# A two-layer hybrid encoder in fp32 products: projections read the tokens interleaved, in a regular order

## The chip, the cores and the metric

The kernel runs on one core of one Trainium2 chip. The metric is the device time of one execution in microseconds (us). The kernel before was run three times: 2403.81, 2404.59 and 2405.13 us, median 2404.59.

## The reference

A trunk of two layers works on one sequence of 256 tokens of width 2048, all in float32. Layer 0 mixes tokens with two recurrences (RWKV-7 heads and an RG-LRU), layer 1 with sparse attention. Around the mixers stand large projections, which are nearly all of the arithmetic:

```python
for layer in range(DEPTH):                       # 2
    if layer % 2 == 0:
        z = x @ ev_w_in[j]                       # 2048 -> 5408
        y = concatenate([rwkv7_mix(z[..., :A_COLS], ...), rglru_mix(z[..., A_COLS:], ...)]) @ ev_w_out[j]
    else:
        y = dsa_mix(x, od_w_in[j], ...) @ od_w_out[j]
    x = layer_norm(DN_ALPHA * x + y, ln1_g[layer], ln1_b[layer])
    x = layer_norm(DN_ALPHA * x + conv_ffn(x, ffn_w_up[layer], ...), ...)   # 2048 -> 11264 -> 5632 -> 2048
    x = x + sigmoid(x @ ple_w_gate[layer]) * (p[layer] @ ple_w_proj[layer])
```

`rwkv7_mix` first shifts by a token: `z = z + (token_shift(z) - z) * mu`, where `token_shift` moves every token one place to the right and puts zero in front. `rglru_mix` and `conv_ffn` begin with a causal depthwise convolution over 4 and 3 tokens. So three consumers of projections look at neighbouring tokens.

## The kernel before

**Layout.** Activations are held transposed: features on the 128 partitions, the S = 256 tokens along the free dimension. A block of 128 features is one tile of 512 numbers, called `x`, `y`, `g` or `o` after the stage: its first 256 columns are the rounded high part of the 256 tokens (type fp32r), its last 256 the low part, which is what the rounding left over. Weights are split in the same way, per chunk of 1024 columns (eight 128x128 blocks): `wchunk` (L117) loads a chunk `raw`, ScalarE writes `hi` (L131), VectorE writes `lo` = raw - hi (L132). In the profile both show at L53, the wrapper that gives them priority.

**Products.** One block of a projection, in float32 accuracy, is three products: high weight by high activation, high weight by low activation, low weight by high activation. `mm3` (L141) issues them in one of two forms.
- As a pair: one matmul of 512 columns, `hi` by the whole tile (L149), whose two halves of sums lie in the two halves of a bank, then one of 256 columns, `lo` by the high part (L150). Here L149 is called H and L150 L. The consumer adds the two halves.
- As a triple, with `one=True`: three matmuls of 256 columns into the same half bank (L145, L146, L147). The consumer finds a finished sum.

Each matmul has its own weight load (LDWEIGHTS) of 128 columns. A row of a projection, 128 output features, is 16 blocks (44 in the down projection) accumulated into one PSUM bank; `gproj` (L171) runs over the row in groups of eight blocks. Banks come from three pools, whose tiles the trace names `pp` and `a`.

**An order by hand.** `dodge` (L152) gives some rows another order of their 32 matmuls, which `ordered` (L164) issues; they stand at L169. In the first such row the second half is eight H, then eight L; in the row after it blocks 12 and 13 are issued H, H, L, L, and all others as pairs. These two rows come after the first five rows of each up projection and again every 29 rows (`DODGE`), after the first five rows of each gate projection, and at the start of the attention output projection.

**Stages.** Layer 0: the input projections in triples, filled with the small matmuls of the recurrences by a scheduler that orders by priority (span to about 380 us); the output projection; LayerNorm. Then, in both layers, the up projection of 88 rows with its convolution and gate (`ffn`, L376), the down projection of 16 rows (L400 to L409), LayerNorm, the gate projection of 16 rows (`ple`, L464). Layer 1 has the attention before that. Right after a LayerNorm, `head` (L219) issues the first five (or three) rows block by block as the normalised tiles arrive.

**Consumers of a bank.** `evac` (L246): ScalarE copies the second half out (L250), VectorE adds the first half to it (L251). `ln_set` and `ln_more` (L267, L276) add a row's sums to the residual. `shifted` (L732) scales a sum on ScalarE (L737) and adds `mu` times its left neighbour on VectorE (L738). `rglru` (L1023) writes the last tap of its convolution on ScalarE (L1028) and adds three more taps on VectorE, reading the bank three times (L1031). Smaller ones are at L447, L451, L480, L1063, L1277, L1322 and L1352.

Of the kernel before, what the change touches and what calls it, by code (L numbers as in the profile page):

```python
# [14 lines left out]
P = 128  # L15
D = 2048
S = 256
# [3 lines left out]
ALPHA = 4.0 ** 0.25  # L21
# [35 lines left out]
class Core:  # L57
# [77 lines left out]
    def hl_split(self, dst, src):  # L135
# [2 lines left out]
        nc.scalar.copy(dst[:, 0:S], src)  # L138
        nc.vector.tensor_tensor(dst[:, S:2 * S], src, dst[:, 0:S].bitcast(F32), op=ALU.subtract)  # L139

    def mm3(self, ps, hi, lo, hl, first, last, one=False):  # L141

        nc = self.nc
        if one:
            nc.tensor.matmul(ps[:, 0:S], hi, hl[:, 0:S], start=first, stop=False)  # L145
            nc.tensor.matmul(ps[:, 0:S], hi, hl[:, S:2 * S], start=False, stop=False)  # L146
            nc.tensor.matmul(ps[:, 0:S], lo, hl[:, 0:S], start=False, stop=last)  # L147
            return
        nc.tensor.matmul(ps[:, 0:2 * S], hi, hl, start=first, stop=False)  # L149
        nc.tensor.matmul(ps[:, 0:S], lo, hl[:, 0:S], start=False, stop=last)  # L150

    def dodge(self, j):  # L152


        self.order = None
        if j in (0, 1):
            o = [(c, k) for k in range(KD) for c in "HL"]
            if j == 0:
                o[16:] = [(c, k) for c in "HL" for k in range(8, KD)]
            else:  # L160
                o[24:28] = [(c, k) for c in "HL" for k in (12, 13)]
            self.order = o

    def ordered(self, ps, hi, lo, hls, k0, order):  # L164

        for what, k in order[2 * k0:2 * k0 + 16]:
            c = slice((k - k0) * P, (k - k0 + 1) * P)
            out, w, x = (ps[:, 0:2 * S], hi, hls[k]) if what == "H" else (ps[:, 0:S], lo, hls[k][:, 0:S])
            self.nc.tensor.matmul(out, w[:, c], x, start=(what, k) == order[0], stop=(what, k) == order[-1], skip_group_check=True)  # L169

    def gproj(self, src, hls, group=8, one=False, more=None):  # L171
# [74 lines left out]
    def evac(self, ps, out):  # L246

        nc = self.nc
        t = self.t("ev")
        nc.scalar.copy(t, ps[:, S:2 * S])  # L250
        nc.vector.tensor_tensor(out, ps[:, 0:S], t, op=ALU.add)  # L251


    def ln_begin(self, new=None):
# [12 lines left out]
    def ln_set(self, m, ps, hl):  # L267

        nc = self.nc
        s = self.sm[m] = self.ln_new(m)  # L270
        t = self.t("lnt")
        nc.vector.scalar_tensor_tensor(s, hl[:, 0:S].bitcast(F32), ALPHA, ps[:, 0:S], op0=ALU.mult, op1=ALU.add)
        nc.vector.scalar_tensor_tensor(t, hl[:, S:2 * S].bitcast(F32), ALPHA, ps[:, S:2 * S], op0=ALU.mult, op1=ALU.add)
        nc.vector.tensor_tensor(s, s, t, op=ALU.add)

    def ln_more(self, m, ps):  # L276

        s = self.sm[m]
        self.nc.vector.tensor_tensor(s, s, ps[:, 0:S], op=ALU.add)

    def ln_stat(self, m):

# [144 lines left out]
    def ple_proj(self, l, wps, phl, half, pool=None):  # L427

        pps, pss = [], [None] * 2
        for m in range(8 * half, 8 * half + 8):  # L430
            wp = wps[m % 8 // 4]
            if pool is None:

                if m % 4 < 2:
                    pss[m % 2] = self.ps()
                ps, n = pss[m % 2], m % 4 // 2
            else:
                if m % 2 == 0:
                    ps = self.ps()
                n = m % 2  # L440
            pv = ps[:, n * S:(n + 1) * S]
            for k in range(2):
                o = ((m % 4) * 2 + k) * P
                self.mm3(pv, wp[0][:, o:o + P], wp[1][:, o:o + P], phl[k], k == 0, k == 1, True)
            if pool is None:
                t = self.t("sp")
                self.nc.scalar.mul(t, pv, 0.5)  # L447
                self.nc.sync.dma_start(self.spill[l][:, (m % 8) * S:(m % 8 + 1) * S], t)
            elif m % 2:
                pp = pool.tile([P, 2 * S], F32, tag="pp", name=self.nm("pp"), bufs=KD // 2)  # L450
                self.nc.scalar.mul(pp, ps, 0.5)  # L451
                pps += [pp[:, 0:S], pp[:, S:]]
        return pps

# [9 lines left out]
    def ple(self, l, pool, new, raws, emit):  # L464

        nc = self.nc
        V = nc.vector
        wps = self.ple_weights(l, 0)
        x, pps, first = self.head(wps, l, 0, [self.a[f"pg{l}"][m] for m in range(FIRST)], f"ln2g{l}", f"ln2b{l}", new, raws, pool)
        pps += self.ple_back(l, pool)  # L470

        def finish(m, ps):

            b = self.t("pl_b")
            pp = pps[m]
            V.tensor_tensor(b, pp, x[m][:, 0:S].bitcast(F32), op=ALU.add)
            V.tensor_tensor(b, b, x[m][:, S:].bitcast(F32), op=ALU.add)
            g = self.t("pl_g")
            if m == KD - 1:
                nc.scalar.activation(g, ps[:, 0:S], AF.Tanh, scale=0.5)  # L480
# [198 lines left out]
class Even:  # L679
# [343 lines left out]
    def rglru(self, j, yout):  # L1023
        nc, k = self.nc, self.k
        V, A, T = nc.vector, nc.scalar, nc.tensor
        ps = yield from k.gproj(k.a["evin"][27 + 2 * j], self.x, one=True)
        xc = self.r1("xc")
        A.activation(xc, ps[:, 0:S], AF.Identity, bias=k.v("bconv_b", j), scale=k.v("bconv3", j))  # L1028
        for n in range(3):
            d = 3 - n  # L1030
            V.scalar_tensor_tensor(xc[:, d:], ps[:, 0:S - d], k.v(f"bconv{n}", j), xc[:, d:], op0=ALU.mult, op1=ALU.add)  # L1031
        bw = self.R.tile([P, 256], F32, tag="bw", name=k.nm("bw"), bufs=1)
        nc.sync.dma_start(bw, k.a["bw"][j])
        rest = k.gproj(k.a["evin"][28 + 2 * j], self.x, one=True)
# [28 lines left out]
        A.activation(g, ps[:, 0:S], AF.Gelu_apprx_tanh)  # L1063
        V.tensor_tensor(h, h, g, op=ALU.mult)
        k.hl_split(yout, h)

# [171 lines left out]
class Odd:  # L1238
# [31 lines left out]
    def index_keys(self):  # L1270
# [6 lines left out]
        A.copy(z, ps[:, 0:S])  # L1277
        yield
        ps = self.a1()
        for i in range(2):  # L1280
# [26 lines left out]
    def low_rank(self, m0, n, gain, name, back=False):  # L1307


        nc, k = self.nc, self.k  # L1310
        V, A = nc.vector, nc.scalar
        zt = self.R.tile([P, 4 * S], F32, tag="bias", name=k.nm("lz"), bufs=2)
        zs = [zt[:, i * S:(i + 1) * S] for i in range(n)]
        acc = k.t("rms")
        for i in range(n):
            g = k.gproj(k.a["odin"][m0 + i], self.x, one=True)
            for _ in range(8):
                next(g)
            yield
            ps = drain(g)  # L1320
            z = zs[i]
            A.copy(z, ps[:, 0:S])  # L1322
            if i == 0:
                A.activation(acc, z, AF.Square)
            else:
                q = k.t("rq")
                A.activation(q, z, AF.Square)
                V.tensor_tensor(acc, acc, q, op=ALU.add)
            yield
        R = k.group_pow(acc, P, 1.0 / (n * P), 1e-6, ALU.add, self.a1, k.t)  # L1330
        yield
        R = k.tok_bcast(R, P, k.t("grb"), "a1")
        out = []
        for i in range(n):
            zn = k.t("zn")
            src, r = zs[i], R[:, 0:S]
            if back:
                src, r = src[:, ::-1], r[:, ::-1]
            V.scalar_tensor_tensor(zn, src, k.v(gain, i), r, op0=ALU.mult, op1=ALU.mult)
            o = self.R.tile([P, 512], F32R, name=f"{name}{i}")  # L1340
            k.hl_split(o, zn)
            out.append(o)
        return out

    def small_proj(self, w, o, hls, out, scale=1.0):
# [6 lines left out]
        nc.scalar.mul(out, ps[:, 0:S], scale)  # L1352

    def scores(self):

# [261 lines left out]
```

## Time and profile before

| | |
|---|---|
| median of three runs | 2404.59 us (2403.81 to 2405.13) |
| span of the profiled execution | 2404.5 us; no other time is recorded for it |
| granted TensorE clock | 1.000 |
| TensorE, matmuls | 2382.8 us busy (99%), 15064 instructions |
| TensorE, weight loads | 2139.0 us (89%) |
| VectorE | 1773.9 us (74%) |
| ScalarE | 1377.4 us (57%) |
| GpSimd | 77.0 us (3%) |
| DMA | 433.77 MB, mean 180 GB/s |

In the rows of the profile "PE" is a matmul and "PEld" a weight load. Matmuls are pipelined: the duration in a row holds the way through the array, so that two of 0.40 and 0.28 us overlap, and what a matmul costs is the distance from its start to the start of the next. A row of the timeline gives start and duration in us, then engine, line, operation, the names of output and inputs, the stationary size, the shape that moves, and how many such instructions it merges. A row of the windows gives a stretch of the span and its length, then for each engine the busy time and in brackets the number of instructions, the granted clock, the share of the DMA engines and GB/s.

### The profile page before, as it was taken

To read this page: it belongs to the slowest core of one execution; us is meant where nothing else is said; L and a number is where in the kernel's file an instruction comes from. 1 tells how busy PE (TensorE), PEld (TensorE's weight loads), DVE (VectorE), ACT (ScalarE), POOL (GpSimd) and SP (SyncE) were. 2 spreads that over 40 slices of the span, in tenths; PEclk is the share of its full clock that TensorE was granted. 3 is DMA by queue.
4 is the path that set the end of the run, shared out by engine and by line. 5 is a ranking of instruction groups with operands and counts; after the bars stand their busy time and mean duration, and the time that the engine had idled before them with its cause. 6 is when DMAs were issued, how large, how long until landed. Compare 5 with 4: busy or idle time off the path is not lost.

```text
span 2404.5 us, 40333 instructions
## 1 busy us (share of the span) xinstructions
PE 2382.8 (99%) x15064; PEld 2139.0 (89%) x15064; DVE 1773.9 (74%) x3598; ACT 1377.4 (57%) x2610; POOL 77.0 (3%) x73
## 2 busy tenths in 40 slices
PE   9999999999999999999999999999999999999999
PEld 8999999888888888888888998888888888888898
DVE  7788888887777777655579598887777777655587
ACT  6777776466555555443356567565555555444354
POOL 0011110000000000000000030000000000000000
PEclk9999999999999999999999999999999999999999
DMA  7444444556665666666666654646666666666665
GB/s 240 145 153 142 139 121 153 174 177 203 191 188 191 191 189 190 185 189 188 189 187 199 188 164 143 214 150 189 191 189 189 192 191 189 183 189 189 192 193 158
DMA packets 137588, 433.77 MB, mean 180 GB/s; under 512 B 16544, under 2 KB 29232, under 8 KB 137392
## 3 DMA queue, kind: packets, MB, share of 16 engines
q1 hardware_dynamic: 137392, 431.19, 57.8%
q8 instruction: 118, 1.93, 0.4%
q14 instruction: 78, 0.64, 0.1%
HBM read 426.65 MB, written 4.48 MB: 179 GB/s over the span
## 4 chain that ended last, share of the span: by engine, by line
PE 88%; DVE 4%; ACT 3%; DMA 3%; issue 1%; POOL 0%; SPq 0%; POOLq 0%; DVEq 0%; ACTq 0%
PE a L149 26%; PE pp L149 18%; PE a L150 13%; PE pp L150 9%; PE pp L145 4%; PE pp L146 4%; PE pp L147 3%; PE a L169 3%; PE a L875 2%; PE pp L169 1%; DMA raw<-evin 1%; ACT hi L53 1%; DVE lo L53 1%; DMA wr<-pg 1%; PE a L145 1%
## 5 line engine op out<-in xcount | busy, mean ns | idle before, releaser
L53 DVE TENSOR_TENSOR lo<-raw,hi 128x1024 fp32r<-128x1024 f32 (+3 forms) x1153 | 976.9, 862 | 464.6 <-ACT hi L53 462.5
L53 ACT CAST hi<-raw 128x1024 fp32r<-128x1024 f32 (+3 forms) x1153 | 840.3, 755 | 697.8 <-PE a L149 305.3
L149 PE MATMUL a<-x,hi 128*128 128x512 f32 x1768 | 619.1, 394 | 2.2 <-DVE x L333 2.2
L150 PE MATMUL a<-x,lo 128*128 128x256 f32 x1768 | 489.6, 277 | 0.0
L149 PEld LDWEIGHTS a<-x,hi 128*128 128x128 f32 x1768 | 331.3, 188 | 79.5 <-DVE x L333 2.9
L149 PE MATMUL pp<-x,hi 128*128 128x512 f32 x1112 | 391.6, 394 | 0.0
L150 PEld LDWEIGHTS a<-x,lo 128*128 128x128 f32 x1768 | 332.0, 188 | 0.3
L150 PE MATMUL pp<-x,lo 128*128 128x256 f32 x1112 | 308.0, 277 | 0.0
L149 PE MATMUL a<-g,hi 128*128 128x512 f32 x836 | 290.4, 394 | 0.0
L149 PEld LDWEIGHTS pp<-x,hi 128*128 128x128 f32 x1112 | 208.5, 188 | 48.5 <-ACT hi L53 0.2
L145 PE MATMUL pp<-x,hi 128*128 128x256 f32 x800 | 239.2, 300 | 1.5 <-ACT x L138 1.2
L150 PE MATMUL a<-g,lo 128*128 128x256 f32 x836 | 231.6, 277 | 0.0
L146 PE MATMUL pp<-x,hi 128*128 128x256 f32 x800 | 226.1, 283 | 0.9 <-DVE x L139 0.9
L147 PE MATMUL pp<-x,lo 128*128 128x256 f32 x800 | 225.9, 283 | 0.0
L392 DVE SCALAR_TENSOR_TENSOR cv<-u,vec_sb,cv 128x255 f32<-128x255 f32 x352 | 169.5, 482 | 64.1 <-ACT cv L389 58.2
L150 PEld LDWEIGHTS pp<-x,lo 128*128 128x128 f32 x1112 | 208.8, 188 | 0.2 <-DVE lo L53 0.2
L149 PEld LDWEIGHTS a<-g,hi 128*128 128x128 f32 x836 | 156.8, 188 | 36.5
L149 PE MATMUL pp<-g,hi 128*128 128x512 f32 x484 | 168.3, 394 | 0.0
L389 ACT ACTIVATE cv<-u,vec_sb 128x256 f32<-128x256 f32 x176 | 105.7, 601 | 93.0 <-DVE u L251 93.0
L150 PEld LDWEIGHTS a<-g,lo 128*128 128x128 f32 x836 | 156.8, 188 | 0.0
L145 PEld LDWEIGHTS pp<-x,hi 128*128 128x128 f32 x800 | 152.8, 191 | 2.9 <-ACT x L138 1.6
L146 PEld LDWEIGHTS pp<-x,hi 128*128 128x128 f32 x800 | 153.0, 191 | 2.1 <-DVE x L139 1.6
(439 smaller groups left out, 3734.9 us busy)
## 6 DMA issues: line engine op xcount, KB each, us to landing
raw<-up SPq DMA_DIRECT2D x347, 512.0 KB, 4.4
raw<-dn SPq DMA_DIRECT2D x160, 512.0 KB, 4.2
raw<-evin SPq DMA_DIRECT2D x85, 512.0 KB, 4.2
raw<-pg SPq DMA_DIRECT2D x54, 512.0 KB, 4.7
raw<-odout SPq DMA_DIRECT2D x32, 512.0 KB, 4.5
raw<-evout SPq DMA_DIRECT2D x16, 512.0 KB, 4.0
raw<-dn SPq DMA_DIRECT2D x32, 256.0 KB, 2.9
raw<-evout SPq DMA_DIRECT2D x16, 448.0 KB, 4.0
```

The lines of the kernel that those rows point to most:

```text
L53: return getattr(self.eng, name)(*args, **kw)
L145: nc.tensor.matmul(ps[:, 0:S], hi, hl[:, 0:S], start=first, stop=False)
L146: nc.tensor.matmul(ps[:, 0:S], hi, hl[:, S:2 * S], start=False, stop=False)
L147: nc.tensor.matmul(ps[:, 0:S], lo, hl[:, 0:S], start=False, stop=last)
L149: nc.tensor.matmul(ps[:, 0:2 * S], hi, hl, start=first, stop=False)
L150: nc.tensor.matmul(ps[:, 0:S], lo, hl[:, 0:S], start=False, stop=last)
L169: self.nc.tensor.matmul(out, w[:, c], x, start=(what, k) == order[0], stop=(what, k) == order[-1], skip_group_check=True)
L389: nc.scalar.activation(y, u, AF.Identity, bias=self.v(f"cb{l}", j), scale=self.v(f"cw2{l}", j))
L392: nc.vector.scalar_tensor_tensor(y[:, d:], u[:, 0:S - d], self.v(f"cw{n}{l}", j), y[:, d:], op0=ALU.mult, op1=ALU.add)
L875: self.nc.tensor.matmul(ps[:, c * P:(c + 1) * P], lhs[:, c * P:(c + 1) * P], rhs(c), start=True, stop=True)
```

## The change

Three helpers describe the same data in another order. `zip` turns the 256 tokens of a part into the order 0, 128, 1, 129, ..., 127, 255; on a whole tile it does so for the high and for the low part. Every projection's matmul takes its moving operand through `zip`, so that it reads two places 512 bytes apart in turn. Tiles stay as they were in SBUF, and the sums are still written to consecutive places of the bank, now in the order in which the tokens were read. `unzip` reads such a bank back with a step of two (all even places, then all odd ones), and `nat` gives an SBUF tile the matching shape of two runs of 128, so that every consumer writes tokens in their natural order again. Matmuls that are no projections (L853 to L1000, L1375 and the like) are not touched.

Two consumers that look at neighbours change more. In `shifted`, token 128 has its left neighbour, 127, at the end of the other run: a new ScalarE instruction of one column per sum adds it, and the VectorE step covers two runs of 127. In `rglru`, ScalarE first copies the sum to a new SBUF tile `u` in natural order, and the four taps read `u` instead of the bank.

Last, `dodge` still makes its list but keeps `None`, so no row is issued by `ordered` and every row takes its products as H, L, H, L.

```diff
+    def zip(self, ap):
+        if ap.shape[1] == S:
+            return ap.rearrange("p (q b) -> p b q", q=2)
+        return ap.rearrange("p (h q b) -> p h b q", h=2, q=2)
+    def unzip(self, ap):
+        return ap.rearrange("p (b q) -> p q b", q=2)
+    def nat(self, ap):
+        return ap.rearrange("p (q b) -> p q b", q=2)
...
         if one:
-            nc.tensor.matmul(ps[:, 0:S], hi, hl[:, 0:S], start=first, stop=False)
+            nc.tensor.matmul(ps[:, 0:S], hi, z(hl[:, 0:S]), start=first, stop=False)
...
-        nc.tensor.matmul(ps[:, 0:2 * S], hi, hl, start=first, stop=False)
-        nc.tensor.matmul(ps[:, 0:S], lo, hl[:, 0:S], start=False, stop=last)
+        nc.tensor.matmul(ps[:, 0:2 * S], hi, z(hl), start=first, stop=False)
+        nc.tensor.matmul(ps[:, 0:S], lo, z(hl[:, 0:S]), start=False, stop=last)
...
-            self.order = o
+            self.order = None
...
         t = self.t("ev")
-        nc.scalar.copy(t, ps[:, S:2 * S])
-        nc.vector.tensor_tensor(out, ps[:, 0:S], t, op=ALU.add)
+        nc.scalar.copy(self.nat(t), self.unzip(ps[:, S:2 * S]))
+        nc.vector.tensor_tensor(self.nat(out), self.unzip(ps[:, 0:S]), self.nat(t), op=ALU.add)
...
-        nc.scalar.mul(out, ps[:, 0:S], self.omu[:, j:j + 1])
-        nc.vector.scalar_tensor_tensor(out[:, 1:], ps[:, 0:S - 1], k.v("mu", j), out[:, 1:], op0=ALU.mult, op1=ALU.add)
+        o, p, mu, h = k.nat(out), k.unzip(ps[:, 0:S]), k.v("mu", j), out[:, P:P + 1]
+        nc.scalar.mul(o, p, self.omu[:, j:j + 1])
+        nc.scalar.activation(h, ps[:, S - 2:S - 1], AF.Identity, scale=mu, bias=h)
+        nc.vector.scalar_tensor_tensor(o[:, :, 1:], p[:, :, 0:P - 1], mu, o[:, :, 1:], op0=ALU.mult, op1=ALU.add)
...
-        A.activation(xc, ps[:, 0:S], AF.Identity, bias=k.v("bconv_b", j), scale=k.v("bconv3", j))
+        u = k.t("u")
+        A.copy(k.nat(u), k.unzip(ps[:, 0:S]))
+        A.activation(xc, u, AF.Identity, bias=k.v("bconv_b", j), scale=k.v("bconv3", j))
         for n in range(3):
             d = 3 - n
-            V.scalar_tensor_tensor(xc[:, d:], ps[:, 0:S - d], k.v(f"bconv{n}", j), xc[:, d:], op0=ALU.mult, op1=ALU.add)
+            V.scalar_tensor_tensor(xc[:, d:], u[:, 0:S - d], k.v(f"bconv{n}", j), xc[:, d:], op0=ALU.mult, op1=ALU.add)
```

The other consumers (`ln_set`, `ln_more`, L447, L451, L480, L1063, L1277, L1322, L1352) only get `nat` and `unzip` around their operands, as in `evac`.

In the program the change shows at two places. The first is TensorE in the up projection of layer 0, at the middle of the first row with an order by hand; `a_1435_7540` is the bank, `x_...` the activation tiles, `hi_...` and `lo_...` the weights. Before:

```order
L169 MATMUL a_1435_7540<-x_7195,hi_7564 128x512
L169 MATMUL a_1435_7540<-x_7210,hi_7564 128x512
L169 MATMUL a_1435_7540<-x_7215,hi_7564 128x512
L169 MATMUL a_1435_7540<-x_7220,hi_7564 128x512
L169 MATMUL a_1435_7540<-x_7225,hi_7564 128x512
L169 MATMUL a_1435_7540<-x_7230,hi_7564 128x512
```

In the changed kernel the same place of the row, now issued by `mm3`, whose lines are 163 and 164 there:

```order
L163 MATMUL a_1443_7583<-x_7238,hi_7607 128x512
L164 MATMUL a_1443_7583<-x_7238,lo_7608 128x256
L163 MATMUL a_1443_7583<-x_7253,hi_7607 128x512
L164 MATMUL a_1443_7583<-x_7253,lo_7608 128x256
L163 MATMUL a_1443_7583<-x_7258,hi_7607 128x512
L164 MATMUL a_1443_7583<-x_7258,lo_7608 128x256
```

Where H followed H, H and L now alternate; the number of matmuls is the same. Outside layer 0's mixer TensorE has no other difference in order. The second place is ScalarE in layer 0's mixer, where the three sums of a head (`kr`, `r`, `v`) are taken from their banks among the other work. Before:

```order
L737 ACTIVATE kr_780<-pp_781,omu 128x256
L53 ACTIVATE kk_893<-kr_780,vec_sb 128x256
L53 COPY akT_922<-a_133_917 128x512
L53 ACTIVATE sq_894<-kk_893 128x256
L53 COPY bd_vb<-a_138_951 64x2x64 x4
```

In the changed kernel:

```order
L752 ACTIVATE kr_786<-pp_787,omu 128x256
L753 ACTIVATE kr_786<-pp_787,kr_786,vec_sb 128x1
L53 COPY akT_929<-a_133_924 128x512
L53 ACTIVATE kk_900<-kr_786,vec_sb 128x256
L53 ACTIVATE sq_901<-kk_900 128x256
```

A one-column instruction follows each of these sums, and a copy has moved ahead of the instruction that needs the finished sum.

More of the change, by code (lines that the diff above doesn't have):

```diff
@@ L139, in hl_split @@
         nc.vector.tensor_tensor(dst[:, S:2 * S], src, dst[:, 0:S].bitcast(F32), op=ALU.subtract)
+    def zip(self, ap):
[6 more added lines that the diff above has]
+        return ap.rearrange("p (q b) -> p q b", q=2)
     def mm3(self, ps, hi, lo, hl, first, last, one=False):
-        nc = self.nc
+        nc, z = self.nc, self.zip
         if one:
-            nc.tensor.matmul(ps[:, 0:S], hi, hl[:, 0:S], start=first, stop=False)
-            nc.tensor.matmul(ps[:, 0:S], hi, hl[:, S:2 * S], start=False, stop=False)
-            nc.tensor.matmul(ps[:, 0:S], lo, hl[:, 0:S], start=False, stop=last)
+            nc.tensor.matmul(ps[:, 0:S], hi, z(hl[:, 0:S]), start=first, stop=False)
+            nc.tensor.matmul(ps[:, 0:S], hi, z(hl[:, S:2 * S]), start=False, stop=False)
+            nc.tensor.matmul(ps[:, 0:S], lo, z(hl[:, 0:S]), start=False, stop=last)
             return
-        nc.tensor.matmul(ps[:, 0:2 * S], hi, hl, start=first, stop=False)
-        nc.tensor.matmul(ps[:, 0:S], lo, hl[:, 0:S], start=False, stop=last)
+        nc.tensor.matmul(ps[:, 0:2 * S], hi, z(hl), start=first, stop=False)
+        nc.tensor.matmul(ps[:, 0:S], lo, z(hl[:, 0:S]), start=False, stop=last)
     def dodge(self, j):
@@ L167, in ordered @@
             c = slice((k - k0) * P, (k - k0 + 1) * P)
-            out, w, x = (ps[:, 0:2 * S], hi, hls[k]) if what == "H" else (ps[:, 0:S], lo, hls[k][:, 0:S])
+            out, w, x = (ps[:, 0:2 * S], hi, self.zip(hls[k])) if what == "H" else (ps[:, 0:S], lo, self.zip(hls[k][:, 0:S]))
             self.nc.tensor.matmul(out, w[:, c], x, start=(what, k) == order[0], stop=(what, k) == order[-1], skip_group_check=True)
@@ L271, in ln_set @@
         t = self.t("lnt")
-        nc.vector.scalar_tensor_tensor(s, hl[:, 0:S].bitcast(F32), ALPHA, ps[:, 0:S], op0=ALU.mult, op1=ALU.add)
-        nc.vector.scalar_tensor_tensor(t, hl[:, S:2 * S].bitcast(F32), ALPHA, ps[:, S:2 * S], op0=ALU.mult, op1=ALU.add)
+        for o, c in ((s, slice(0, S)), (t, slice(S, 2 * S))):
+            nc.vector.scalar_tensor_tensor(self.nat(o), self.nat(hl[:, c].bitcast(F32)), ALPHA, self.unzip(ps[:, c]), op0=ALU.mult, op1=ALU.add)
         nc.vector.tensor_tensor(s, s, t, op=ALU.add)
     def ln_more(self, m, ps):
-        s = self.sm[m]
-        self.nc.vector.tensor_tensor(s, s, ps[:, 0:S], op=ALU.add)
+        s = self.nat(self.sm[m])
+        self.nc.vector.tensor_tensor(s, s, self.unzip(ps[:, 0:S]), op=ALU.add)
     def ln_stat(self, m):
@@ L446, in ple_proj @@
                 t = self.t("sp")
-                self.nc.scalar.mul(t, pv, 0.5)
+                self.nc.scalar.mul(self.nat(t), self.unzip(pv), 0.5)
                 self.nc.sync.dma_start(self.spill[l][:, (m % 8) * S:(m % 8 + 1) * S], t)
@@ L450, in ple_proj @@
                 pp = pool.tile([P, 2 * S], F32, tag="pp", name=self.nm("pp"), bufs=KD // 2)
-                self.nc.scalar.mul(pp, ps, 0.5)
+                self.nc.scalar.mul(pp.rearrange("p (n q b) -> p n q b", n=2, q=2), ps.rearrange("p (n b q) -> p n q b", n=2, q=2), 0.5)
                 pps += [pp[:, 0:S], pp[:, S:]]
@@ L479, in finish @@
             if m == KD - 1:
-                nc.scalar.activation(g, ps[:, 0:S], AF.Tanh, scale=0.5)
+                nc.scalar.activation(self.nat(g), self.unzip(ps[:, 0:S]), AF.Tanh, scale=0.5)
             else:
@@ L1062, in rglru @@
         g = self.r1("g")
-        A.activation(g, ps[:, 0:S], AF.Gelu_apprx_tanh)
+        A.activation(k.nat(g), k.unzip(ps[:, 0:S]), AF.Gelu_apprx_tanh)
         V.tensor_tensor(h, h, g, op=ALU.mult)
@@ L1276, in index_keys @@
         z = k.t("kz")
-        A.copy(z, ps[:, 0:S])
+        A.copy(k.nat(z), k.unzip(ps[:, 0:S]))
         yield
@@ L1321, in low_rank @@
             z = zs[i]
-            A.copy(z, ps[:, 0:S])
+            A.copy(k.nat(z), k.unzip(ps[:, 0:S]))
             if i == 0:
@@ L1351, in small_proj @@
             k.mm3(ps, w[0][:, o + i * P:o + (i + 1) * P], w[1][:, o + i * P:o + (i + 1) * P], hls[i], i == 0, i == n - 1, True)
-        nc.scalar.mul(out, ps[:, 0:S], scale)
+        nc.scalar.mul(k.nat(out), k.unzip(ps[:, 0:S]), scale)
     def scores(self):
```

## The prediction, as put on record

> **What bounds the kernel now.** I first read the page's busy times and its chain of waits.
>
> ```profile
> PE 2382.8 (99%) x15064; PEld 2139.0 (89%) x15064; DVE 1773.9 (74%) x3598; ACT 1377.4 (57%) x2610; POOL 77.0 (3%) x73
> PE 88%; DVE 4%; ACT 3%; DMA 3%; issue 1%; POOL 0%; SPq 0%; POOLq 0%; DVEq 0%; ACTq 0%
> core 0: 2404.5 us, clock 1.000
> ```
>
> TensorE is busy 99% of the span, carries 88% of the chain that ended last, and runs at the full granted clock. So only the distance between matmuls can move the time by much. The windows by stage say how tight it is: layer 0's mixer, then an up projection, then part of a down projection.
>
> ```profile
> 0.00:380.00 380.00, 369.52 (x2986) 361.28 (x2987) 314.31 (x1024) 275.09 (x742) 46.74 (x46) 1.00 0.50 158
> 560.00:680.00 120.00, 120.00 (x695) 104.94 (x694) 87.65 (x133) 69.73 (x110) 0.00 (x0) 1.00 0.61 193
> 900.00:1200.00 300.00, 300.00 (x1732) 262.24 (x1731) 181.82 (x248) 136.96 (x179) 0.00 (x0) 1.00 0.63 188
> ```
>
> In the down projection 1732 matmuls, 866 pairs H and L, fill 300 us without a gap: 346.4 ns per pair. In the mixer TensorE idles 10.5 of 380 us.
>
> Next, what a matmul's step is made of. The timeline of a stretch of triples in layer 1, its first and last row (15 matmuls lie between the two starts):
>
> ```profile
> 2290.10 0.28 PE L145 MATMUL pp<-g,hi 128*128 128x256 f32 x1
> ...
> 2291.90 0.28 PE L145 MATMUL pp<-g,hi 128*128 128x256 f32 x1
> ```
>
> 1.80 us for 15 gives 120 ns for 256 columns. If a step is c per column plus a fixed o, triples say 256c + o = 120 and pairs 768c + 2o = 346.4; so 256c = 106.4 ns and o = 13.6 ns. Every projection matmul pays 13.6 ns beyond its columns, whatever its width.
>
> Now the same matmul in plain fp32, which the recurrences use; each such product shows as two instructions (x2):
>
> ```profile
> 45.75 0.60 PE L817 MATMUL a<-g,lora 128*128 128x256 f32 x2
> 46.19 0.59 PE L818 MATMUL a<-g,lora 128*128 128x256 f32 x2
> 46.62 0.59 PE L824 MATMUL a<-rk,cst_sb 128*128 128x256 f32 x2
> ```
>
> Starts 0.435 us apart, so 217.5 ns for an instruction of 256 columns. That is 2 x 106.4 + 4.7: columns at half the pace, and a fixed part of 4.7 ns, a third of 13.6. These instructions load as many weights. So the fixed part is not the price of loading or swapping weights; it appears when columns are read at full pace, as if the weight load and the moving read meet on the way from SBUF and the moving read loses 8.9 ns each time.
>
> A third observation fits that. Right after a LayerNorm pairs are slower, here in the last gate projection (six pairs between the two starts):
>
> ```profile
> 2316.77 0.40 PE L149 MATMUL a<-x,hi 128*128 128x512 f32 x1
> ...
> 2318.89 0.40 PE L149 MATMUL a<-x,hi 128*128 128x512 f32 x1
> ```
>
> 2.12 us for six is 353.3 ns a pair, steadily, with no wait: the fixed part is 17.0 ns there. It is the irregular rows that end it, by the timeline of the second such row in layer 0:
>
> ```profile
> 535.39 0.63 PE L169 MATMUL pp<-x,hi 128*128 128x512 f32 x2
> 535.86 0.39 PE L169 MATMUL pp<-x,lo 128*128 128x256 f32 x2
> ...
> 536.78 0.40 PE L149 MATMUL a<-x,hi 128*128 128x512 f32 x1
> ...
> 541.98 0.39 PE L149 MATMUL a<-x,hi 128*128 128x512 f32 x1
> ```
>
> After H, H, L, L, from 536.78 to 541.98 us, 15 pairs take 5.20 us, 346.7 ns each, and this pace then holds. The same instructions have two paces, by the phase in which weight loads and moving reads fall. So the order by hand buys 353.3 - 346.4 = 6.9 ns a pair.
>
> **The change, part by part.**
>
> *Reading order.* It touches every projection matmul. Their numbers, from the windows of lines 149, 169 and 145 (each line's rows before and after 380 us; line 150 has as many as 149):
>
> ```profile
> 380.00:2404.50 2024.50, 1670.70 (x4800) 899.82 (x4800) 1.00 0.60 185
> 380.00:2404.50 2024.50, 104.83 (x576) 87.91 (x576) 1.00 0.60 185
> 0.00:380.00 380.00, 206.40 (x688) 131.19 (x688) 1.00 0.50 158
> 380.00:2404.50 2024.50, 135.27 (x464) 88.23 (x464) 1.00 0.60 185
> ```
>
> That is 4800 pairs and 576/2 = 288 irregular ones, 5088 in all; triples 688 x 3 = 2064 matmuls in the mixer and 464 x 3 = 1392 later. No matmul of the trace reads single elements from two places in turn, so the new step has to be bounded. From below: the fixed part shrinks to the 4.7 ns of plain fp32, because each of the two places is read only every other column. A second floor is the weight load itself, from the 32-column matmuls of a LayerNorm, whose columns take next to nothing:
>
> ```profile
> 2301.74 0.50 PE L304 MATMUL a<-cst_sb,acc 128*128 128x32 f32 x3
> 2302.07 0.36 PE L145 MATMUL a<-p,hi 128*128 128x256 f32 x1
> ```
>
> Three in 0.33 us, 0.11 us for each load, which I take as 112 ns with the rounding. So a 256-column step ends at 112 and a 512-column step at 2 x 106.4 + 4.7 = 217.5; a pair at about 330. From above: each element from another place costs a whole access, as if at the pace of plain fp32: 217.5 for 256 columns and 430 for 512, a pair 648 ns.
>
> The step is thus between 330 and 648, against 346.4. I take 330: the rows show that two paces exist for one and the same work by phase alone, and that reading each place at half pace is what takes the fixed part from 13.6 to 4.7. The gain is 16.4 ns x 5088 = 83.4 us, and 8 ns x 1392 = 11.1 us of triples. In the mixer 8 x 2064 = 16.5 us would be saved on TensorE, but the 10.5 us of idleness there say that other engines are late at places; I take half, 8.3. Together 102.8 us.
>
> [...]
>
> *Irregular rows gone.* If the phase no longer matters this costs nothing. If it does, it is the first rival.
>
> *Reading banks with a step of two.* No long row of the trace reads PSUM so. The rows of the evacuation, and the nearest strided read, a VectorE sum over 256 elements 64 bytes apart, beside a plain sum over 256:
>
> ```profile
> L250 ACT COPY ev<-a 128x256 f32<-128x256 f32 x129 | 47.1, 365 | 6.4 <-PE a L150 6.4
> L251 DVE TENSOR_TENSOR u<-a,ev 128x256 f32<-128x256 f32 x110 | 46.0, 418 | 1.2 <-ACT ev L250 1.2
> L53 DVE TENSOR_REDUCE y<-dblk 128x64 f32<-128x256 f32 x8 | 4.7, 589 | 0.0
> L1463 DVE TENSOR_REDUCE sm<-L 128x1 f32<-128x256 f32 x16 | 6.5, 408 | 0.0
> ```
>
> The bounds are zero and a doubling (+0.37 and +0.42 us); the strided sum is longer by 0.18, and I take that. In an up projection VectorE is busy 87.65 of 120 us and ScalarE 69.73, over 21.7 rows; even the doubling adds 9 and 8 us, which TensorE covers at the shorter 114 us too. It shows only where a LayerNorm or the end waits for the last sums: four LayerNorms and the last gate row, one or two reads each, 0.18 to 0.84 apiece; I take 2 us in all.
>
> *Small instructions.* A one-column ScalarE instruction is priced by the row of a one-column copy, the copy of `rglru` by L250:
>
> ```profile
> L85 ACT COPY cst_sb<-g 128x1 f32<-128x1 f32 x1 | 0.2, 191 | 0.0
> ```
>
> 27 x 0.191 + 8 x 0.365 = 8.1 us on ScalarE, in a mixer where it is busy 275 of 380 us. VectorE's step at L738 now waits for one instruction more on ScalarE's queue; behind it on VectorE stand the `lo` of coming weights, for which six buffers give room. Three of the 27 stand on the way to the first head, where nothing fills: 3 x 0.19 = 0.6, taken as 1 us. The others cost up to 8 us if that cover is gone.
>
> The sum: -102.8 + 2 + 1 = -99.8. The profiled execution's span is 2404.5 and the median of the runs 2404.59, so both are one: **2305 us**.
>
> **The rivals.**
>
> *The pace stays and the bad phase returns.* If the reading order changes nothing for TensorE, removing the irregular rows leaves it in the phase in which each stage starts. For it: the five rows after a LayerNorm at 353.3 ns are regular ones, and nothing but an irregular row is seen to end that phase. Against it: the phase depends on the pattern of reads, which changes. About 300 of the 5088 pairs run slow already; 4800 x 6.9 = 33 us, and 3 us of small costs: 2440 us. It decides as soon as the fixed part with the new order is 13.6 ns or more in the starting phase. Chance 0.20.
>
> *Each element costs an access.* Then pairs take 648 ns and triples 217.5 a step: 301.6 x 5088 + 97.5 x 3456 = 1871 us more, 4276 us. For it: consecutive elements lie 512 bytes apart. Against it: a load and a moving read do meet now, so the path has no such wide reserve that single reads must break it, and I see no row for it. [...] Chance 0.08.
>
> *Half the way.* The collisions become fewer but not none, fixed part 9 ns: half the gain, 2355 us. Chance 0.20.
>
> *No net effect.* The paces differ, but by as much as small costs and the lost order give back, within 0.2% (5 us), which is what a measurement of this kernel can tell from no change: 2400 to 2409. Chance 0.07.
>
> *More collisions*, a pair at 360 ns: +69 us, 2475. Chance 0.05.
>
> **How the numbers follow.** The forecast of 2305 has 0.40. Faster: 0.40 + 0.20 = 0.60; same 0.07; slower 0.20 + 0.08 + 0.05 = 0.33. The low end: all of the mixer's 16.5 us, no small costs, and 111 for 112 ns in the loads, 2404.5 - 83.4 - 11.1 - 16.5 - 8.5 = 2285. The range reaches to the first rival's 2440 and holds 0.40 + 0.20 + 0.07 + most of 0.20. The forecast's own range is 2285 to 2330.
>
> **What would show it.** Right: in a down projection 300 us hold some 1818 matmuls instead of 1732, from the first rows after a LayerNorm on, and a triple steps at 112 ns. First rival: 353.3 ns a pair through whole stages. [...] The consumers are wrongly priced if L250 or L251 doubles. The prediction is wrong if the pair's step is not below 346 ns.

## The result, and the profile after

The changed kernel takes 2308.33 us (median of four runs, 2307.21 to 2309.31) against 2404.86 us for the kernel before: ratio 0.9598, 95% interval 0.9584 to 0.9612. The prediction was 2305. In the profiled execution the span is 2306.7 us, 97.8 less than before.

The page's busy times, the chain and the clock of the changed kernel:

```profile
PE 2267.7 (98%) x15064; PEld 2105.7 (91%) x15064; DVE 1772.4 (77%) x3598; ACT 1384.2 (60%) x2646; POOL 81.4 (4%) x73
PE 79%; DVE 8%; ACT 6%; DMA 5%; issue 1%; POOL 1%; SPq 0%; POOLq 0%; DVEq 0%; ACTq 0%
core 0: 2306.7 us, clock 0.999
```

The same 15064 matmuls, at a granted clock of 0.999 against 1.000, are busy for 115 us less (2267.7 against 2382.8). VectorE and ScalarE do as much as before, and a larger part of the chain now runs through them. The windows by stage: the mixer, an up projection, and two stretches that hold nothing but pairs (here L163 is H, L164 is L).

```profile
0.00:380.00 380.00, 359.96 (x2987) 347.97 (x2988) 314.75 (x1024) 284.20 (x778) 51.01 (x46) 1.00 0.50 158
560.00:680.00 120.00, 120.00 (x734) 110.29 (x734) 94.70 (x143) 75.30 (x119) 0.00 (x0) 1.00 0.65 210
900.00:1150.00 250.00, 250.00 (x1529) 229.90 (x1528) 159.20 (x217) 118.34 (x152) 0.00 (x0) 1.00 0.67 200
600.00:900.00 300.00, 300.00 (x1834) 275.89 (x1833) 231.49 (x347) 183.14 (x290) 0.00 (x0) 1.00 0.64 204
```

In 300 us there are now 917 pairs, 327.2 ns each, where 346.4 stood before. Two timelines answer the other rows of the prediction: the pairs right after the last LayerNorm, first and last of eight, and triples of layer 1, first and last of twelve matmuls.

```profile
2221.74 0.38 PE L163 MATMUL pp<-x,hi 128*128 128x512 f32 x1
...
2224.36 0.38 PE L163 MATMUL a<-x,hi 128*128 128x512 f32 x1
```

```profile
2194.99 0.28 PE L159 MATMUL pp<-g,hi 128*128 128x256 f32 x1
...
2196.33 0.28 PE L159 MATMUL pp<-g,hi 128*128 128x256 f32 x1
```

2.62 us for eight pairs is 327.5 ns: the slow pace of 353.3 that the kernel before had at this place is gone. 1.34 us for twelve is 112 ns a matmul of a triple, against 120.

### The profile page after: what moved, and what is told of

Read it like the earlier page. It is cut to its first block, busy times and chain, and to the rows that moved or that the text cites. A ratio compares the mean times of both kernels' runs of the same rounds, so it can differ in the third digit from the quotient of the medians.

```text
span 2306.7 us, 40380 instructions
## 1 busy us (share of the span) xinstructions
PE 2267.7 (98%) x15064; PEld 2105.7 (91%) x15064; DVE 1772.4 (77%) x3598; ACT 1384.2 (60%) x2646; POOL 81.4 (4%) x73
## 4 chain that ended last, share of the span: by engine, by line
PE 79%; DVE 8%; ACT 6%; DMA 5%; issue 1%; POOL 1%; SPq 0%; POOLq 0%; DVEq 0%; ACTq 0%
PE a L163 27%; PE pp L163 19%; PE a L164 13%; PE pp L164 9%; DVE lo L53 2%; ACT hi L53 2%; PE pp L159 2%; DMA raw<-evin 2%; PE pp L160 2%; PE pp L161 2%; PE a L891 1%; DMA raw<-evout 1%; DMA raw<-up 1%; POOL gr L378 0%; DVE s L344 0%
## 5 line engine op out<-in xcount | busy, mean ns | idle before, releaser
L163 PE MATMUL a<-x,hi 128*128 128x512 f32 x1960 | 648.9, 382 | 2.7 <-DVE x L347 2.7
L164 PE MATMUL a<-x,lo 128*128 128x256 f32 x1960 | 533.7, 273 | 0.0
L163 PEld LDWEIGHTS a<-x,hi 128*128 128x128 f32 x1960 | 370.3, 189 | 54.7 <-DVE x L347 2.2
L163 PE MATMUL pp<-x,hi 128*128 128x512 f32 x1176 | 392.4, 382 | 1.7 <-ACT pp L465 1.6
L164 PEld LDWEIGHTS a<-x,lo 128*128 128x128 f32 x1960 | 376.3, 192 | 0.1
L164 PE MATMUL pp<-x,lo 128*128 128x256 f32 x1176 | 320.4, 273 | 0.0
L163 PE MATMUL a<-g,hi 128*128 128x512 f32 x836 | 274.4, 382 | 0.0
L163 PEld LDWEIGHTS pp<-x,hi 128*128 128x128 f32 x1176 | 222.3, 189 | 33.3 <-ACT pp L465 2.2
L159 PE MATMUL pp<-x,hi 128*128 128x256 f32 x800 | 233.2, 292 | 2.3 <-DVE la L754 2.0
L164 PE MATMUL a<-g,lo 128*128 128x256 f32 x836 | 227.9, 273 | 0.0
L164 PEld LDWEIGHTS pp<-x,lo 128*128 128x128 f32 x1176 | 225.7, 192 | 0.2 <-DVE lo L53 0.2
L160 PE MATMUL pp<-x,hi 128*128 128x256 f32 x800 | 221.0, 276 | 1.4 <-DVE x L139 1.4
L161 PE MATMUL pp<-x,lo 128*128 128x256 f32 x800 | 220.7, 276 | 1.6 <-DVE lo L53 1.6
L163 PEld LDWEIGHTS a<-g,hi 128*128 128x128 f32 x836 | 158.0, 189 | 22.0
L164 PEld LDWEIGHTS a<-g,lo 128*128 128x128 f32 x836 | 160.5, 192 | 0.0
L163 PE MATMUL pp<-g,hi 128*128 128x512 f32 x484 | 159.1, 382 | 0.0
L159 PEld LDWEIGHTS pp<-x,hi 128*128 128x128 f32 x800 | 153.7, 193 | 3.4 <-DVE la L754 2.2
L160 PEld LDWEIGHTS pp<-x,hi 128*128 128x128 f32 x800 | 154.0, 192 | 2.7 <-DVE x L139 2.1
```

Source lines behind the costliest of these rows:

```text
L159: nc.tensor.matmul(ps[:, 0:S], hi, z(hl[:, 0:S]), start=first, stop=False)
L160: nc.tensor.matmul(ps[:, 0:S], hi, z(hl[:, S:2 * S]), start=False, stop=False)
L161: nc.tensor.matmul(ps[:, 0:S], lo, z(hl[:, 0:S]), start=False, stop=last)
L163: nc.tensor.matmul(ps[:, 0:2 * S], hi, z(hl), start=first, stop=False)
L164: nc.tensor.matmul(ps[:, 0:S], lo, z(hl[:, 0:S]), start=False, stop=last)
```

## The experiments

All pair times below are read in one way, from a window of 250 us (900 to 1150 us of the span) that holds pairs only: 250 us divided by half of its matmuls. The kernel before has 1444 there, 346.3 ns a pair; the changed kernel 1529, 327.0. The window of the kernel before:

```profile
900.00:1150.00 250.00, 250.00 (x1444) 218.56 (x1443) 154.46 (x213) 116.26 (x156) 0.00 (x0) 1.00 0.63 189
```

### What the irregular rows did

The kernel before, all rows regular (`b_regular`):

```diff
-            self.order = o
+            self.order = None
```

> The kernel before, with the irregular rows made regular and nothing else. Phase theory: TensorE stays at 353 ns a pair after every LayerNorm, 2404.5 + 33 = 2437 us (ratio 1.014). Rival (the irregular rows bought nothing once a stage runs): 346.4 ns a pair and 2404 us, ratio 1.000.

Measured: 2432.32 us, ratio to the kernel before 1.0089 (1.0054 to 1.0123). The window of its pairs:

```profile
900.00:1150.00 250.00, 250.00 (x1417) 216.85 (x1416) 152.96 (x211) 115.35 (x156) 0.00 (x0) 1.00 0.61 184
```

352.9 ns a pair, in the middle of a long run of rows. The phase theory holds in the main; so half of the change, made alone, costs time. Its size was a little less than 33 us, 25.5 by the medians. But an irregular row isn't the only way out of the slow pace. The gate projection of layer 0 has the fast one in this run, though all of its rows are regular (80 pairs lie between the two starts):

```profile
1285.38 0.39 PE L149 MATMUL pp<-x,hi 128*128 128x512 f32 x1
...
1313.12 0.39 PE L149 MATMUL pp<-x,hi 128*128 128x512 f32 x1
```

27.74 us for 80 is 346.8 ns a pair. And of the four executions three took 2431.5 to 2434.0 us and one 2415.4; there is no trace of that one, but a larger share of pairs at the fast pace would explain it. So this kernel, which reads in natural order, differed by 16 to 19 us between executions, and the totals of the single runs below are to be read with that in mind.

The other half alone, the changed kernel with the irregular rows back (`a_irregular`):

```diff
-            self.order = None
+            self.order = o
```

> The changed kernel, with the irregular rows put back. Theory (with two places in turn no phase is left to lose): 327.5 ns a pair with or without them, 2308 us within 3. Rival (a phase still matters, and the irregular rows move it): rows after the first irregular one run at another pace, up to 7 ns a pair either way, 2275 or 2341 us.

Measured: 2308.55 us, ratio 0.9593 (0.9573 to 0.9613), the same as the changed kernel's. With the new reading order the irregular rows neither gain nor lose (0.2 us), and there is no need for an order by hand.

### What the consumers cost

The changed kernel with natural reads and everything else kept (`read_plain`):

```diff
     def zip(self, ap):
-        if ap.shape[1] == S:
-            return ap.rearrange("p (q b) -> p b q", q=2)
-        return ap.rearrange("p (h q b) -> p h b q", h=2, q=2)
+        return ap
```

> The changed kernel with the moving operand read in natural order; consumers still read with a step of two, so tokens land in another order than the reference's. If the step-of-two reads and the small instructions cost little: as the kernel before without irregular rows, plus 3 us (2440 us if that one is 2437). If they carry a hidden cost: more than 10 us above it.

Measured: 2434.73 us (2433.23 and 2436.23), ratio 1.0114 (1.0094 to 1.0135), 2.4 us above `b_regular`, which is no more than the executions of one kernel differ by. All of the gain comes from the order of reading; the reads with a step of two and the added instructions cost a few us at most.

### What about the order matters

Four kernels differ from the changed one in `zip` alone; of each, only the new lines are shown. Neighbours swapped within groups of four (`read_0213`):

```diff
+        return ap.rearrange("p (a b q) -> p a q b", b=2, q=2)
```

> Moving operand read 0, 2, 1, 3, 4, 6, 5, 7, ...: every group of four stays in its 16 bytes; the bank's consumers are unchanged, so tokens land in another order than the reference's. Shape theory (any pattern that is not one run of neighbours removes the fixed part): a pair 328 ns, 2308 us. Lane theory (odd and even reads go through two lanes, each of which fetches its own 16 bytes; interleaving helps because each lane then walks through neighbours): each lane still fetches every 16 bytes for two elements, fixed part 13.6 to 17 ns, a pair 346 to 353, 2405 to 2440 us.

Measured: 2434.86 us, one run. Its window is that of natural reading, 352.9 ns a pair:

```profile
900.00:1150.00 250.00, 250.00 (x1417) 216.70 (x1417) 152.03 (x210) 115.61 (x156) 0.00 (x0) 1.00 0.61 185
```

So a pattern of several dimensions, or one that isn't a run of neighbours, is not what helps. The shape theory falls.

Two neighbouring groups of four in turn (`read_near`):

```diff
+        return ap.rearrange("p (a q b) -> p a b q", q=2, b=4)
```

> Moving operand read 0, 4, 1, 5, 2, 6, 3, 7, 8, 12, ...: two neighbouring groups of 16 bytes in turn; consumers unchanged, so tokens land in another order than the reference's. Lane theory and shape theory: a pair 328 ns, 2308 us. Distance theory (the two places must lie far apart, in other parts of the memory): 346 to 353 ns a pair, 2405 to 2440 us.

Measured: 2305.34 us, one run, 327.0 ns a pair:

```profile
900.00:1150.00 250.00, 250.00 (x1529) 229.94 (x1528) 158.21 (x213) 117.25 (x151) 0.00 (x0) 1.00 0.67 200
```

Two places 16 bytes apart serve as well as two that lie 512 bytes apart (327.0 ns a pair in both). The distance theory falls, and the halves of the token range have no part in it.

Sixteen places in turn (`read_16`), and a single run with a step of two (`read_step2`):

```diff
+            return ap.rearrange("p (q b) -> p b q", q=16)
+        return ap.rearrange("p (h q b) -> p h b q", h=2, q=16)
```

```diff
+            return ap.rearrange("p (b q) -> p q b", q=2)
+        return ap.rearrange("p (h b q) -> p h q b", h=2, q=2)
```

> Moving operand read 0, 16, 32, ..., 240, 1, 17, ...: sixteen places in turn; consumers unchanged, so tokens land in another order than the reference's. Lane theory: every read needs a fetch of its own, up to the pace of plain fp32, a pair 648 ns, about 4280 us. Shape theory: a pair 328 ns, 2308 us.

> Moving operand read 0, 2, 4, ..., 254, 1, 3, ...: one run with a step of two; consumers unchanged, so tokens land in another order than the reference's. Lane theory: each lane finds one element per 16 bytes, every read fetches, up to 648 ns a pair, about 4280 us. Theory that counts elements per 16 bytes without lanes: two per fetch instead of four, between 346 and 400 ns a pair, 2405 to 2680 us. Shape theory: 328 ns, 2308 us.

Measured: 4316.46 us and 4460.95 us, one run each. The window of `read_16`, then that of `read_step2`:

```profile
900.00:1150.00 250.00, 250.00 (x759) 156.45 (x758) 95.16 (x141) 76.85 (x119) 0.00 (x0) 1.00 0.31 99
```

```profile
900.00:1150.00 250.00, 250.00 (x729) 151.31 (x728) 93.01 (x138) 73.50 (x115) 0.00 (x0) 1.00 0.30 95
```

658.8 and 685.9 ns a pair, half the pace. The six orders together:

| order of reading | every second read finds in 16 bytes | ns a pair | us |
|---|---|---|---|
| 0, 1, 2, 3, ... (`b_regular`) | 2 elements | 352.9 | 2432.3 |
| 0, 2, 1, 3, ... | 2 | 352.9 | 2434.9 |
| 0, 4, 1, 5, ... | 4 | 327.0 | 2305.3 |
| 0, 128, 1, 129, ... (the change) | 4 | 327.0 | 2308.3 |
| 0, 16, 32, ... | 1 | 658.8 | 4316.5 |
| 0, 2, 4, ... | 1 | 685.9 | 4461.0 |

The lane theory, written down ahead of these runs, gave the side on which each falls, though the last two came out above the 648 ns and 4280 us that it named: take every second read for a stream of its own, count how many of its elements lie in one group of 16 bytes, and the pace follows. Four gave 327.0 ns a pair, two cost 10 to 13 ns more per matmul (346.3 or 352.9 a pair), one halved the pace (658.8 and 685.9). The size of the group comes out of the runs as well: in groups of 8 bytes 0, 2, 1, 3 would count like 0, 4, 1, 5, and in groups of 32 so would the natural order, but their pairs are 25.9 ns apart. No run shows what in the hardware does this, two lanes or something else; the rule is what was measured, on six orders. Why a step of two is 4% slower than sixteen places isn't explained by it.

### Whether the weight loads are to blame

The prediction held that the lost time is where a weight load and a moving read meet. Three kernels ask that. The kernel before with regular rows and weight loads that take every eighth column (`weights_step8`):

```diff
-                self.mm3(ps, hi[:, k * P:(k + 1) * P], lo[:, k * P:(k + 1) * P], hls[k0 + k],
+                self.mm3(ps, hi[:, k::kn], lo[:, k::kn], hls[k0 + k],
```

> The kernel before with regular rows, and in the loop over a projection's row the weight loads take every eighth column of a chunk instead of 128 neighbours; the sums mix other weights than the reference's. Collision theory (the fixed part is where a weight load's fetches meet the moving read): 128 fetches a load instead of 32, fixed part well above 13.6 to 17 ns, up to 54, a pair 370 to 430, 2500 to 2800 us. Rival (the fixed part belongs to the start of a moving read, whatever the load does): 346 to 353 ns a pair, as without the edit.

Measured: 3367.34 us, one run, above both ranges. A window that holds pairs only, from the up projection into the down projection, says why:

```profile
1300.00:1500.00 200.00, 200.00 (x825) 200.00 (x826) 93.44 (x133) 73.60 (x104) 0.00 (x0) 1.00 0.43 133
```

485 ns a pair, with the weight loads busy all the time: two loads of 242 ns, over twice the 0.11 us of a plain one. The loads became the bound, so the run doesn't answer the question. It shows that a load of every eighth column is slower, 242 ns against 0.11 us; why isn't shown.

The low-weight load of each pair cut to 32 columns (`load_32`):

```diff
-        nc.tensor.matmul(ps[:, 0:2 * S], hi, hl, start=first, stop=False)
-        nc.tensor.matmul(ps[:, 0:S], lo, hl[:, 0:S], start=False, stop=last)
+        nc.tensor.matmul(ps[:, 0:2 * S], hi, hl, start=first, stop=last, skip_group_check=True)
+        nc.tensor.matmul(ps[0:32, 0:S], lo[:, 0:32], hl[:, 0:S], start=False, stop=last, skip_group_check=True)
```

> The kernel before with regular rows, and the low-weight matmul of every pair loads 32 columns of weights instead of 128 (it computes 32 of its 128 features). Collision theory: that load meets the moving read a quarter as often, so the fixed parts of a pair fall by three eighths, from 27 to 34 down to 17 to 21 ns, a pair 336 to 341 ns, 2350 to 2380 us; and it falls in the step of the 512-column matmul, under which that load runs. Rival (start of a moving read): 346 to 353 ns a pair, 2405 to 2440 us.

Measured: 2418.00 us, one run, and 349.7 ns a pair, in the rival's range. That is 3 ns below the slow pace of the full loads and 3 ns above their fast one, so alone it doesn't part a shorter load from another phase:

```profile
900.00:1150.00 250.00, 250.00 (x1430) 162.80 (x1428) 152.94 (x211) 115.83 (x155) 0.00 (x0) 1.00 0.62 187
```

Both loads of all blocks but the first and last of a row cut so (`load_32_all`); the core of the edit, in `mm3`:

```diff
+        def mm(h, w, x, start, stop):
+            n = P if first or last else 32
+            nc.tensor.matmul(ps[0:n, h], w[:, 0:n], x, start=start, stop=stop, skip_group_check=True)
```

> The kernel before with regular rows; in every block of a projection's row but the first and the last, all matmuls load 32 columns of weights instead of 128, and compute 32 of 128 features. Collision theory (the fixed part is the price of the loads' fetches): it falls by three quarters in these blocks, to 3.4 to 4.3 ns, a pair near 328 and a triple's step near 110 ns, 2310 to 2330 us. Start theory (reading in natural order, each fetch serving two reads of each lane, leaves no slack, and every matmul pays when it begins): 13.6 to 17 ns stay, a pair 346 to 353 ns, 2400 to 2435 us. A mixture, by what one short load of the pair took off (3.7 ns): 342 to 346 ns, 2380 to 2400 us.

Measured: 2388.79 us, one run:

```profile
900.00:1150.00 250.00, 250.00 (x1456) 161.40 (x1454) 155.19 (x214) 116.39 (x155) 0.00 (x0) 1.00 0.63 190
```

343.4 ns a pair, in the mixture's range, and below both paces of the full loads. For 768 columns the prediction's equations give 3 x 106.4 = 319.2 ns; by that estimate the fixed part of a matmul is 16.9 or 13.6 ns with full loads (352.9 or 346.3 a pair), 12.1 with loads a quarter as wide, and 3.9 with the interleaved order and full loads.

Which of the full loads' two paces is 343.4 to be compared with? This run, too, has a second pace, in the attention output projection (80 pairs between the two starts):

```profile
1469.82 0.39 PE L146 MATMUL pp<-o,hi 128*32 128x512 f32 x1
...
1497.68 0.39 PE L146 MATMUL pp<-o,hi 128*32 128x512 f32 x1
```

27.86 us for 80 is 348.3 ns. If 348.3 and 343.4 are the slow and the fast pace of 352.9 and 346.3, short loads took off 4.6 and 2.9 ns a pair, so 1.5 to 2.3 ns a matmul. Only if 343.4 were the slow pace would it be 5. The loads' width is thus worth a small part of the 10 to 13 ns that the new order takes off with full loads; what else of a load or of plain reading makes up the rest isn't shown. Nor do these runs show how the loads' width has its small effect.

The estimates rest on equations that let every matmul pay the same. The rows with eight H, then eight L, give the step of each kind by itself. The kernel before, then `a_irregular`:

```profile
528.36 2.00 PE L169 MATMUL a<-x,hi 128*128 128x512 f32 x8
530.20 1.11 PE L169 MATMUL a<-x,lo 128*128 128x256 f32 x8
```

```profile
525.92 1.89 PE L183 MATMUL a<-x,hi 128*128 128x512 f32 x8
527.65 1.05 PE L183 MATMUL a<-x,lo 128*128 128x256 f32 x8
```

From the first H to the first L are 1.84 and 1.73 us for eight H: 230 ns in natural order, 216 interleaved. The order takes 14 ns off an H, and 216 is 3 ns above the 212.8 that the equations give for 512 columns, near the 3.9.

### Who pays, and the mixer

The changed kernel with the 256-column matmul of a pair in natural order (`zip_H`):

```diff
-        nc.tensor.matmul(ps[:, 0:S], lo, z(hl[:, 0:S]), start=False, stop=last)
+        nc.tensor.matmul(ps[:, 0:S], lo, hl[:, 0:S], start=False, stop=last)
```

> The changed kernel, with the 256-column matmul of a pair reading in natural order; its sums land on other tokens than the reference's. Theory (each matmul pays for its own plain reading): 218 + 117 to 120 ns, a pair 336 to 338, about 2308 + 45 = 2353 us. Rival (the load pays or the pair as a whole, so that one interleaved partner is enough): 328 ns, 2308 us, or both parts back: 346 ns.

Measured: 2335.16 us, one run, 332.9 ns a pair:

```profile
900.00:1150.00 250.00, 250.00 (x1502) 229.51 (x1502) 157.62 (x215) 117.78 (x153) 0.00 (x0) 1.00 0.65 196
```

Six ns over the changed kernel, a part of what both in natural order cost (19 to 26). That is between the rival's 328 and the theory's 336 to 338, and 2335 us between their 2308 and 2353, so neither forecast was met. The rival's two forms fall: one interleaved partner isn't enough, and one plain reader doesn't bring both parts back. That each matmul pays for its own reading alone isn't shown, as the pair lost less than that asks for. The starts in the trace, averaged from 1000 to 1050 us, would put it on the interleaved partner: from L to H are 118 ns against 109 in the changed kernel, from H to L 215 against 218. How far starts can part the two matmuls of a pair is itself not known.

Last, the input projections of layer 0 and their consumers put back (`zip_outside`). Beside the old lines of `shifted` and `rglru`, this is:

```diff
-        nc, z = self.nc, self.zip
+        nc, z = self.nc, (lambda t: t) if flat else self.zip
...
-            ps = yield from k.gproj(k.a["evin"][m], self.x, one=True)
+            ps = yield from k.gproj(k.a["evin"][m], self.x, one=True, flat=True)
```

> The changed kernel, with the input projections of layer 0 and their consumers (shift, RG-LRU) as in the kernel before; all other projections read interleaved. Theory A (in the mixer the shorter step of the triples buys nothing, since other engines set its pace): mixer as long as in the changed kernel or shorter by some us of ScalarE work, total 2304 to 2309 us. Theory B (the shorter step does help there, and the added ScalarE instructions ate it only in part): triples back at 120 ns cost up to 2064 x 8 ns = 16 us, total 2312 to 2324 us.

Measured: 2307.08 us, ratio 0.9584 (0.9569 to 0.9598), no different from the changed kernel's 0.9598 (0.9584 to 0.9612). Theory A holds. The stretch up to the first LayerNorm, in the kernel before, the changed one and this one, shows where the shorter step went:

```profile
0.00:485.60 485.60, 473.33 (x3640) 453.96 (x3641) 403.92 (x1274) 335.64 (x892) 48.99 (x48) 1.00 0.50 158
```

```profile
0.00:481.30 481.30, 458.21 (x3640) 438.96 (x3640) 402.25 (x1268) 343.31 (x925) 53.26 (x48) 1.00 0.51 159
```

```profile
0.00:478.60 478.60, 467.88 (x3640) 452.34 (x3640) 401.31 (x1268) 334.16 (x889) 48.96 (x48) 1.00 0.50 160
```

3640 matmuls each. From before to after TensorE's busy time falls by 15.1 us, and its idle time rises from 12.3 to 23.1 us: 4.3 us reach the end of the stretch. With the mixer as it was, TensorE idles 10.7 us and the stretch is 2.7 us shorter still. So interleaving buys nothing there. The added ScalarE instructions alone don't make TensorE wait: `read_plain` has them and idles 9.8 us up to its first LayerNorm (window 0 to 485.1 us). That the order of the mixer's work on VectorE and ScalarE sets the pace is the reading that fits; no run changed that order alone.

## Why the prediction was right

- **What bounds the kernel.** Right. After the first LayerNorm TensorE has no gaps in the long stages, before or after, and the gain came out of the step between matmuls. The window from 900 to 1200 us that the prediction calls a down projection begins in the up projection, which ends near 985 us; as both run at the same pace, 346.4 ns stands.
- **The step.** Forecast 330 ns a pair and 112 ns in a triple, measured 327.2 and 112. A triple stands at the floor of 112 that I set by the load's length. Whether the floor binds in a pair too isn't shown: 327.2 less the 216 of an H in a row of eight leaves 111 for L.
- **Why the step shrinks.** Half wrong. The prediction put the lost time on weight loads that meet moving reads, and took the relief from each place being read every other column. That was my reading of 13.6 against 4.7 ns; no run shows a load and a read meeting. Loads of a quarter of the width took off some 2 of 10 to 13 ns; an interleaving that stays within 16 bytes took off nothing, one of two neighbouring groups took off all. In the six orders measured, the pace follows how many elements each of two alternating streams gets from 16 bytes. So it is luck that the bound from plain fp32, 4.7 ns, was near the 3.9 that the windows give by the same equations: it was argued from something else.
- **The slow pace.** The prediction saw nothing but an irregular row end it. `b_regular` has a stretch at the fast pace without one.
- **The mixer.** Mis-sized. Half of 16.5 us was put down as saved. Up to the first LayerNorm only 4.3 us came through. The 232 pairs of the output projection in that stretch account for that by themselves (232 x 19.2 ns = 4.5 us), and `zip_outside` shows that the triples' shorter step gave none of it.
- **The sum.** Its terms were further off than 2305 against 2308 shows. The pairs gave more than forecast: 19.2 ns x 5088 = 97.7 us for 83.4. The mixer gave nothing for 8.3: the 4.3 us up to the first LayerNorm, less 4.5 for the output projection's pairs, are -0.2. And TensorE waits longer behind the other engines. The stretch from the first LayerNorm to the end, before, after and in `read_plain`:

```profile
485.60:2404.50 1918.90, 1909.51 (x11426) 1685.05 (x11425) 1369.96 (x2324) 1041.72 (x1719) 28.02 (x25) 1.00 0.60 186
```

```profile
481.30:2306.70 1825.40, 1809.53 (x11424) 1666.78 (x11424) 1370.13 (x2331) 1040.93 (x1722) 28.18 (x25) 1.00 0.63 196
```

```profile
485.10:2434.50 1949.40, 1939.58 (x11425) 1699.68 (x11424) 1370.66 (x2324) 1039.43 (x1719) 28.01 (x25) 1.00 0.58 183
```

  TensorE's idle time there rises by 6.5 us, from 9.4 to 15.9, where the prediction allowed 2. `read_plain`, which has the changed consumers and the longer step, idles 9.8 us, so it is the shorter step that lays these waits bare. The waits that are new lie at a gate projection, a LayerNorm and the attention (us in total, times, longest):

```profile
PE pp L163 <- ACT pp L465: 1.6, 1, 1.6
PE pp L320 <- DVE s L293: 1.2, 1, 1.2
PE a L1443 <- DVE L L1447: 1.0, 1, 1.0
```

  With the triples at the forecast 11.1, these terms make 97.7 + 11.1 - 0.2 - 6.5 = 102.1 us, 4 more than the 97.8 measured between the two traces; those 4 us have no account here. So it is luck that errors of up to 14 us cancel to 3.
- **Reading with a step of two.** Forecast +0.18 us for each such read. The rows of the changed kernel:

```profile
L264 ACT COPY ev<-a 128x256 f32<-128x256 f32 x129 | 47.1, 365 | 4.4 <-PE a L164 4.4
L753 ACT ACTIVATE v<-pp,v,vec_sb 128x1 f32<-128x1 f32 x8 | 2.8, 353 | 0.1
```

```profile
L265 DVE TENSOR_TENSOR u<-a,ev 128x256 f32<-128x256 f32 x110 | 46.0, 418 | 0.0
```

  365 and 418 ns, as before to the nanosecond: it costs nothing. The strided VectorE row that I priced it by (589 ns against 408) was not a fit pattern: it writes 64 sums where the other writes one maximum, and what made it longer isn't shown.
- **Small instructions.** A column of `shifted` takes 0.35 us, not the 0.19 of a copy: it also reads a scale and a bias, and its bank, and which of these costs the time isn't shown. 27 of them are 9.5 us on ScalarE. They show once on TensorE by name, at the first head (us in total, times, longest):

```profile
PE pp L159 <- DVE la L754: 2.0, 1, 2.0
```

  Before, TensorE waited 0.2 us for that step. The total of side costs, 3 us forecast, was 2.4 by `read_plain`, within the spread of the executions; the longer waits of the changed kernel (see the sum) come on top.
- **First rival (bad phase).** Rightly kept apart: the irregular rows were worth 25 us, and would have been lost had the order not paid.
- **Second rival (each element costs an access).** Given 0.08 and priced at 648 ns a pair. In 0, 128, 1, 129 every element lies some 510 bytes from the one before, and the pair took 327.0, so the measurement decides against it for this order. But there are orders that cost about what the rival was priced at: `read_16` runs at 659 and `read_step2` at 686.

## What to carry to other kernels

Where fp32r matmuls follow each other without a wait, look at the start-to-start distance less the columns' time; if some 13 to 17 ns are left per matmul (by the estimate above), read the moving operand as two streams in turn, each through neighbours (0, 4, 1, 5, ... is enough), and undo the order when the bank is read, which cost nothing here; consumers that look at neighbours need a few instructions more. A step of two, or sixteen places in turn, halved the pace here (685.9 and 658.8 ns a pair). In a stage whose pace other engines set, leave the order as it is: in the mixer here the new one saved nothing (2307.08 us without it there, 2308.33 with it).

## What the runs showed of the hardware

- The moving read: by the estimate above 3.9 ns of fixed cost per matmul when every second read finds four fp32r elements in 16 bytes (327.0 ns a pair), 13.6 to 16.9 when it finds two (346.3 to 352.9), and half the pace when it finds one (658.8 to 685.9).
- With natural reading there are two steady paces, 346.3 and 352.9 ns a pair, for one and the same sequence of instructions; reordered rows switch it (`b_regular` against the kernel before), and in `b_regular` it changed without them (346.8 ns in a gate projection). With interleaved reading of both matmuls only one was seen (327.0 to 327.5 ns).
- A weight load of every eighth column takes 242 ns instead of 111.
- ScalarE and VectorE read a PSUM bank with a step of two elements as fast as without (365 and 418 ns for 256 columns, before and after).

Still open: what in the hardware makes the two paces, why a step of two is slower than sixteen places, why a pair with one plain reader lost less than half of what two lost, and what makes up the part of the fixed cost that the loads' width doesn't.
